# Five more norms take their rows by way of DRAM: memory, x, first feed-forward, between the blocks, second feed-forward

## The chip, the core and the metric

The kernel runs on one core of a Trainium2 chip. The metric is the device time of one execution in microseconds (us). The engines of the core are PE (TensorE, matrix products into PSUM), DVE (VectorE), ACT (ScalarE), POOL (GpSimd) and SP (SyncE, here a queue of weight loads). ACT and POOL issue DMAs too, each on its own queue. Every engine works through its instructions in a fixed order and waits on semaphores.

## The reference

Two transformer blocks over 512 rows of 1024 values in float32, one batch. The first block has a mixer (attention and a gated recurrence), cross attention to 256 memory rows and a feed-forward; the second has a gated convolution, a state-space branch and a gated feed-forward. Each part begins with an RMS norm, and this is the piece that matters here:

```python
def rmsnorm(x, g):
    xf = x.astype(jnp.float32)
    y = xf * lax.rsqrt(jnp.mean(xf * xf, axis=-1, keepdims=True) + EPS)
    return (y * g.astype(jnp.float32)).astype(x.dtype)
```

Five of these norms are touched: that of the memory, that of x at the start, the one ahead of the first feed-forward, the one between the blocks, and the one ahead of the second feed-forward.

## The kernel before

Activations lie transposed in SBUF: 128 of the 1024 columns on the partitions, the 512 rows along the free axis, eight tiles for one activation. A product in float32 is made of three matmuls in a reduced format, of the high and low parts of both sides: `mm3`, L150 to L152. A tile of a product, `gemm_tile`, is 8 column blocks x 3 = 24 matmuls of 128x512 into one PSUM slot of the pool `acc`, which has three slots. Weights come on SP's queue into `wr` (three buffers); ACT casts the high part `wh` (L138), DVE subtracts to get the low part `wl` (L139), and PE uses both. The cast of a later weight waits for PE to finish the tile that used the buffer.

A norm's factor is needed as a row: the scale of row r stands in column r of R, the same on all partitions, since DVE multiplies tiles of 128x512 by it. ACT squares the tiles and DVE adds them (`sqa`); PE sums over the partitions with one-column products (`col_sum`, L234), so that the sums of 512 rows stand as four columns of 128; DVE scales them (`rv`, L240) and POOL takes the power -1/2 (`rc`, L242). Then there are two ways from four columns to a row on all partitions:

- `row_bc` (L245 to L251): one 128x128 matmul per column against the identity (L249), then an ACT copy from PSUM to R.
- `row_far` (L253 on): one small transpose on PE (L256), an ACT copy to `rt` (L258), a DMA on ACT's queue to DRAM, `rd` (L260), and a DMA on POOL's queue that reads it back to all 128 partitions.

`row_far` is already used for the mixer's and the state-space branch's norms (their rows are Rh and Rg); the five norms of this case use `row_bc`.

In the products that follow a norm in the two feed-forwards the activations go in unnormed, since a row's factor can be applied to the product; so PE may start such tiles before R is there, and DVE multiplies the tile in PSUM by R when it reads it (L715, L1207, L1211). That read gives the PSUM slot back. For the x norm DVE multiplies h itself by R (L335), then ACT casts its high part xh and DVE makes its low part xl (L212, L213), and PE needs these.

The order of each engine is fixed at build by a scheduler: `tc.high_priority(-n)` lets instructions stand later in the order than their place in the code; `LATE`, `X2`, `X3` and the like are such numbers. `tc.issue_after(x)` holds an instruction behind another one.

In the second feed-forward the norm is made in two halves of 256 rows (`r3(cl, w)` over `parts`), each with its own column sums and row.

## Time and profile before

| | |
|---|---|
| time, median of 3 runs | 1896.86 us (1894.96 to 1898.19) |
| profiled execution, its own time | 1897.12 us |
| its span | 1895.3 us |
| around the span | 1.8 us |
| mean granted clock of PE, as a share of full speed | 0.998 |
| busy: PE, DVE, ACT, POOL | 1876.6, 1192.4, 843.7, 134.2 us |

The span reaches from the first instruction to the last of one profiled execution. Busy time is the sum of the instructions of an engine; a PE that is busy for nearly the whole span can only be made faster by taking work from it or by filling its gaps.

### The profile page before, as it was taken

Reading aid. Unit: us, or ns where it says so; the run is one execution under the profiler, and the core shown is the slowest. Engines: PE = TensorE matmul, PEld = TensorE weight load, DVE = VectorE, ACT = ScalarE, POOL = GpSimd, SP = SyncE. Lnnn points to the kernel's source line nnn. Section 1 sums busy time; section 2 is a strip of 40 time slices with the busy share of each in tenths; the row PEclk is TensorE's granted clock in tenths of the full one; section 3 lists DMA queues with packets and bytes.
Section 4 is the critical chain, followed back from the end, with each engine's and each line's share of the span. In section 5 each row is a group of like instructions: output and inputs, shape, how many; then the busy total and the mean of one; then the engine's idle time right before and its main releaser. Section 6 shows DMA issues by size and latency. Waiting matters only on the chain.

```text
span 1895.3 us, 24243 instructions
## 1 busy us (share of the span) xinstructions
PE 1876.6 (99%) x9313; PEld 1546.5 (82%) x9313; DVE 1192.4 (63%) x1837; ACT 843.7 (45%) x1364; POOL 134.2 (7%) x251
## 2 busy tenths in 40 slices
PE   9999999999999999999999999999999999999998
PEld 8787776878888888877888888888888998888887
DVE  6744756665442344467889889579998675423444
ACT  6524547444431243348545653445335553322231
POOL 1001110000000000011100110100000014000000
PEclk9999999999999999999999999999999999999999
DMA  7312222312233223334333433333345446223331
GB/s 259 137 56 101 67 79 73 106 56 89 89 100 98 93 99 111 108 92 132 126 109 123 124 128 100 115 102 123 105 139 188 153 133 177 93 97 100 97 103 67
DMA packets 65435, 210.65 MB, mean 111 GB/s; under 512 B 8884, under 2 KB 10720, under 8 KB 65320
## 3 DMA queue, kind: packets, MB, share of 16 engines
q1 hardware_dynamic: 52384, 177.27, 29.1%
q0 software_dynamic: 8672, 24.47, 4.6%
q10 hardware_dynamic: 4264, 7.37, 1.1%
q8 instruction: 73, 1.20, 0.3%
q14 instruction: 42, 0.34, 0.1%
HBM read 198.45 MB, written 10.66 MB: 110 GB/s over the span
## 4 chain that ended last, share of the span: by engine, by line
PE 93%; DVE 3%; DMA 1%; ACT 1%; issue 1%; POOL 0%; SPq 0%; DVEq 0%; POOLq 0%; ACTq 0%
PE acc L150 26%; PE acc L152 26%; PE acc L151 26%; PE pb L960 1%; PE pa L490 1%; PE pa L150 1%; PE pa L152 1%; PE pb L150 1%; PE pb L152 1%; PE pa L151 1%; PE pb L151 1%; PE pb L585 1%; PE pa L930 1%; DMA wr<-w_xk 1%; PE pb L557 1%
## 5 line engine op out<-in xcount | busy, mean ns | idle before, releaser
L138 ACT CAST wh<-wr 128x1024 fp32r<-128x1024 f32 x313 | 328.7, 1051 | 701.1 <-PE acc L151 512.7
L139 DVE TENSOR_TENSOR wl<-wr,wh 128x1024 fp32r<-128x1024 f32 x313 | 382.9, 1224 | 290.8 <-ACT wh L138 288.6
L150 PE MATMUL acc<-yh,wh 128*128 128x512 f32 (+1 forms) x1112 | 432.6, 389 | 0.4 <-DVE so L1008 0.3
L152 PE MATMUL acc<-yh,wl 128*128 128x512 f32 (+1 forms) x1112 | 431.5, 388 | 0.0
L151 PE MATMUL acc<-yl,wh 128*128 128x512 f32 (+1 forms) x1112 | 429.7, 386 | 0.0
L152 PE MATMUL acc<-xh,wl 128*128 128x512 f32 (+1 forms) x832 | 314.2, 378 | 0.3 <-DVE wl L139 0.3
L150 PE MATMUL acc<-xh,wh 128*128 128x512 f32 (+1 forms) x832 | 313.3, 378 | 0.3 <-DVE h L628 0.3
L151 PE MATMUL acc<-xl,wh 128*128 128x512 f32 (+1 forms) x832 | 313.4, 377 | 0.0
L150 PEld LDWEIGHTS acc<-yh,wh 128*128 128x128 f32 x1112 | 209.4, 188 | 42.4 <-issue 1.4
L152 PEld LDWEIGHTS acc<-yh,wl 128*128 128x128 f32 x1112 | 209.4, 188 | 42.1 <-issue 1.5
L151 PEld LDWEIGHTS acc<-yl,wh 128*128 128x128 f32 x1112 | 209.3, 188 | 41.4 <-issue 0.6
L851 DVE SCALAR_TENSOR_TENSOR cv<-gp,vec,cv 128x512 f32<-128x512 f32 x240 | 178.2, 750 | 5.9 <-ACT cv L849 3.0
L152 PEld LDWEIGHTS acc<-xh,wl 128*128 128x128 f32 x832 | 157.1, 189 | 28.8 <-issue 2.4
L150 PEld LDWEIGHTS acc<-xh,wh 128*128 128x128 f32 x832 | 156.8, 189 | 28.4 <-ACT xh L212 0.9
L151 PEld LDWEIGHTS acc<-xl,wh 128*128 128x128 f32 x832 | 156.9, 189 | 27.0 <-issue 1.3
L150 PE MATMUL acc<-uh,wh 128*128 128x512 f32 x256 | 99.6, 389 | 0.0
L151 PE MATMUL acc<-ul,wh 128*128 128x512 f32 x256 | 99.6, 389 | 0.0
L152 PE MATMUL acc<-uh,wl 128*128 128x512 f32 x256 | 99.6, 389 | 0.0
L715 DVE SCALAR_TENSOR_TENSOR t<-acc,R 128x512 f32<-128x512 f32 x32 | 22.0, 691 | 79.4 <-PE acc L152 78.5
L242 POOL TENSOR_TENSOR rc<-rv,mhalf 128x4 f32<-128x4 f32 (+2 forms) x19 | 23.5, 1235 | 606.2 <-DVE rv L240 521.0
L152 PEld LDWEIGHTS acc<-uh,wl 128*128 128x128 f32 x256 | 48.1, 188 | 10.0
L151 PEld LDWEIGHTS acc<-ul,wh 128*128 128x128 f32 x256 | 48.1, 188 | 9.9
(433 smaller groups left out, 2448.1 us busy)
## 6 DMA issues: line engine op xcount, KB each, us to landing
wr<-w SPq DMA_DIRECT2D x64, 512.0 KB, 3.7
wr<-w_gu SPq DMA_DIRECT2D x44, 512.0 KB, 3.4
wr<-w_out SPq DMA_DIRECT2D x24, 512.0 KB, 3.5
wr<-w_dn SPq DMA_DIRECT2D x22, 512.0 KB, 3.4
wr<-w_xs SPq DMA_DIRECT2D x16, 512.0 KB, 3.5
wr<-w_glu SPq DMA_DIRECT2D x16, 512.0 KB, 3.6
ab<-acsd POOLq DMA_DIRECT2D x32, 256.0 KB, 3.8
wr<-w_z SPq DMA_DIRECT2D x16, 512.0 KB, 4.1
```

What stands on the lines that cost most here:

```text
L138: A.copy(out=hi[:, :n], in_=raw[:, :n])
L139: V.tensor_tensor(out=lo[:, :n], in0=raw[:, :n], in1=hi[:, :n].bitcast(F32), op=ALU.subtract)
L150: T.matmul(out=ps, lhsT=lh, rhs=rh, start=start, stop=False)
L151: T.matmul(out=ps, lhsT=lh, rhs=rl, start=False, stop=False)
L152: return T.matmul(out=ps, lhsT=ll, rhs=rh, start=False, stop=stop)
L242: G.tensor_tensor(out=r[:, :nt], in0=v[:, :nt], in1=mhalf[:, :nt], op=ALU.pow)
L490: T.matmul(out=ps[:, j * 64:(j + 1) * 64], lhsT=k_[:, j * P:(j + 1) * P], rhs=qv[:, j, :, 1, :], start=True, stop=True)
L557: T.transpose(out=pt[:, i * P:(i + 1) * P], in_=Sx[:, i * P:(i + 1) * P], identity=ident)
L585: m = T.matmul(out=ps, lhsT=fq[p][es_, sl], rhs=fk[p][es_, 0:n], start=True, stop=True)
L715: V.scalar_tensor_tensor(out=t, in0=ps, scalar=0.0, in1=R, op0=ALU.max, op1=ALU.mult)
L851: yield V.scalar_tensor_tensor(out=o, in0=gp[:, t:t + S], scalar=cw(t), in1=o, op0=ALU.mult, op1=ALU.add)
L930: T.matmul(out=ps[:, 0:256], lhsT=Bt[:, c, :], rhs=xw[:, c].rearrange("p r d -> p (r d)"), start=True, stop=True)
```

## The change

Five places go from `row_bc` to `row_far` or to a way like it.

- Memory: `Rm` comes by `row_far` with two columns.
- x: `norm_fin` has an argument `far`, and is called with it here.
- First feed-forward: the column sums stand earlier in the order (`FARL` in place of `LATE`), and the transpose is held behind the fifth mark of the first tile (`first_tile`).
- Between the blocks: the transpose of `r1` and its DMA to DRAM (`rows1`) stand at the start of a much earlier part; where R1 is needed, a DMA on ACT's queue reads it back.
- Second feed-forward: the two halves become one norm over all four columns, by `row_far`.

The cross attention's norm is written anew with `norm_col`, and still uses `row_bc`.

```diff
--- before.py
+++ after.py
@@ -36,6 +36,7 @@
 LATE2 = 15
 LATE3 = 100
 X0 = 10
+FARL = 10
 RMARK = 3
 X1 = 0
 X2 = 30
@@ -258,26 +259,39 @@
         A.copy(out=t[0:nt], in_=ps[0:nt, 0:P])
         d = dram.tile([8, P], F32, tag="rd", name="rd", bufs=4)
         nc.scalar.dma_start(out=d[0:nt], in_=t[0:nt])
+        n = nt // len(dst)
         for i, x in enumerate(dst):
-            G.dma_start(out=x, in_=d[4 * i:4 * i + 4].rearrange("a b -> (a b)").unsqueeze(0).partition_broadcast(P))
+            G.dma_start(out=x, in_=d[n * i:n * i + n].rearrange("a b -> (a b)").unsqueeze(0).partition_broadcast(P))
         return dst
 
-    def norm(srcs, n, nt, gain=None, eps=EPS, pl=None, rtag="R", ms=mA, late=0):
-
-        ac = nrm.tile([P, S], F32, tag="sqa", name="sqa")
-        for k, s in enumerate(srcs):
-            sq_acc(ac[:, :nt * P], k, s, 1.0 if gain is None else gain(k))
-        return norm_fin(ac, n, nt, eps, pl, rtag, ms, late)
-
-    def norm_fin(ac, n, nt, eps=EPS, pl=None, rtag="R", ms=mA, late=0):
+    def norm_fin(ac, n, nt, eps=EPS, pl=None, rtag="R", ms=mA, late=0, far=False):
 
         pl = pl or nrm
         R = pl.tile([P, nt * P], F32, tag=rtag, name=rtag, bufs=1)
         with tc.high_priority(-late):
             r = rsqrt_col(col_sum(ac, nt, ms), nt, n, eps)
         with tc.high_priority(-2 * late):
-            A.copy(out=R, in_=row_bc(r, nt, ms))
+            if far:
+                row_far(r, nt, [R], ms)
+            else:
+                A.copy(out=R, in_=row_bc(r, nt, ms))
         return R, r
+
+    def norm_col(srcs, ms, late):
+
+        ac = nrm.tile([P, S], F32, tag="sqa", name="sqa")
+        for k, s in enumerate(srcs):
+            sq_acc(ac, k, s)
+        with tc.high_priority(-late):
+            return rsqrt_col(col_sum(ac, 4, ms), 4, D)
+
+    def first_tile(src, xs, r, R, ms):
+
+        marks = []
+        ps = gemm_tile(src, xs, marks=marks)
+        with tc.issue_after(marks[4].ins):
+            row_far(r, 4, [R], ms)
+        return ps
 
     emem = es_mem
 
@@ -323,13 +337,13 @@
         with tc.high_priority(400):
             rm = rsqrt_col(col_sum(ac, 2), 2, D)
         with tc.high_priority(-X3):
-            A.copy(out=Rm, in_=row_bc(rm, 2))
+            row_far(rm, 2, [Rm])
         ax = nrm.tile([P, S], F32, tag="sqa", name="sqa")
         for k in range(8):
             sq_acc(ax, k, h[k])
         for n in range(8):
             V.tensor_tensor(out=mk[n // 2][:, n % 2, :], in0=mk[n // 2][:, n % 2, :], in1=Rm, op=ALU.mult)
-        R, rc = norm_fin(ax, D, 4, pl=pmx, late=X3)
+        R, rc = norm_fin(ax, D, 4, pl=pmx, late=X3, far=True)
         xs = []
         for k in range(8):
             V.scalar_tensor_tensor(out=h[k], in0=h[k], scalar=vcol("norm_mix_g", k), in1=R, op0=ALU.mult, op1=ALU.mult)
@@ -642,7 +656,10 @@
         pc = ec.enter_context(pool("pc", 2, reuse_waits="tile"))
         pcy = ec.enter_context(pool("pcy", 8, reuse_waits="tile"))
         xs = [split_act(h[k], vcol("norm_x_g", k)) for k in range(8)]
-        R, _ = norm(h, D, 4, pl=pc, ms=mC, late=LATE)
+        R = pc.tile([P, S], F32, tag="R", name="R", bufs=1)
+        r = norm_col(h, mC, LATE)
+        with tc.high_priority(-2 * LATE):
+            A.copy(out=R, in_=row_bc(r, 4, mC))
         ys = []
 
         def split(t, lpool, ltag, lbufs, tag, bufs):
@@ -706,11 +723,13 @@
         pc = ec.enter_context(pool("pff", 2, reuse_waits="tile"))
         ph2 = ec.enter_context(pool("phid", 16, reuse_waits="tile"))
         xs = [split_act(h[k], vcol("norm_ff_g", k)) for k in range(8)]
-        R, _ = norm(h, D, 4, pl=pc, ms=mC, late=LATE)
+        R = pc.tile([P, S], F32, tag="R", name="R", bufs=1)
+        r = norm_col(h, mC, FARL)
         for grp in range(2):
             hid = []
             for n in range(16):
-                ps = gemm_tile([(a["w1"][grp * 16 + n], 8)], xs)
+                src = [(a["w1"][grp * 16 + n], 8)]
+                ps = gemm_tile(src, xs) if grp + n else first_tile(src, xs, r, R, mC)
                 t = pc.tile([P, S], F32, tag="t", name="t")
                 V.scalar_tensor_tensor(out=t, in0=ps, scalar=0.0, in1=R, op0=ALU.max, op1=ALU.mult)
                 t2 = pc.tile([P, S], F32, tag="t2", name="t2")
@@ -1008,6 +1027,14 @@
                 V.tensor_tensor(out=so[n], in0=so[n], in1=ps, op=ALU.add)
                 V.scalar_tensor_tensor(out=so[n], in0=t, scalar=1.0, in1=so[n], op0=ALU.add, op1=ALU.mult)
 
+
+    rows1 = dram.tile([4, P], F32, tag="rows1", name="rows1")
+    with tc.high_priority(-LATE3):
+        ps = mC()
+        T.transpose(out=ps[0:4, 0:P], in_=r1, identity=ident)
+        t = nrm.tile([8, P], F32, tag="sq", name="rt")
+        A.copy(out=t[0:4], in_=ps[0:4, 0:P])
+        nc.scalar.dma_start(out=rows1, in_=t[0:4])
     early = []
     for i, w in enumerate(ew):
         ps = gemm_tile([(w, 8)], xr) if i else eps_[0]
@@ -1080,7 +1107,7 @@
         nc.sync.dma_start(out=t, in_=hd_[k])
         h.append(t)
     R1 = pt_.tile([P, S], F32, tag="Rm", name="R1", bufs=1)
-    A.copy(out=R1, in_=row_bc(r1, 4))
+    nc.scalar.dma_start(out=R1, in_=rows1.rearrange("a b -> (a b)").unsqueeze(0).partition_broadcast(P))
     for n in range(8):
         ps = gemm_tile([(a["w_pw"][n], 8)], cs_)
         t = pt_.tile([P, S], F32, tag="pw", name="pw")
@@ -1116,14 +1143,15 @@
             V.scalar_tensor_tensor(out=xs[k][1][:, cl], in0=h[k][:, cl], scalar=g, in1=xs[k][0][:, cl].bitcast(F32),
                                    op0=ALU.mult, op1=ALU.subtract)
 
-    def r3(cl, w):
+    def r3():
         ac = nrm.tile([P, S], F32, tag="sqa", name="sqa")
-        for k in range(8):
-            sq_acc(ac[:, :w], k, h[k][:, cl])
+        for cl in parts:
+            for k in range(8):
+                sq_acc(ac[:, cl], k, h[k][:, cl])
         with tc.high_priority(-X2):
-            r = rsqrt_col(col_sum(ac[:, :w], w // P), w // P, D)
+            r = rsqrt_col(col_sum(ac, 4), 4, D)
         with tc.high_priority(-2 * X2):
-            A.copy(out=R3[:, cl], in_=row_bc(r, w // P))
+            row_far(r, 4, [R3])
 
     acs = out2(parts[0], HF)
     x3(parts[0], HF, acs, X0)
@@ -1157,8 +1185,7 @@
         for n, ps in zip(order, gu_tiles(order[:3]) + [gemm_tile([(a["w_gu"][n], 8)], xs) for n in order[3:NEARLY]]):
             early[n] = act.tile([P, S], F32, tag="xl", name="early")
             A.copy(out=early[n], in_=ps)
-        for cl in parts:
-            r3(cl, HF)
+        r3()
 
         def gu(n):
             return early[n] if n in early else gemm_tile([(a["w_gu"][n], 8)], xs)
```

How the instructions stand, at three places. First DVE at the x norm. Before (h0 to h2 are tiles of x, R is the x norm's row, `vec` the gains, Rm the memory's row, mk the memory's keys):

```order
L331 TENSOR_TENSOR mk_136<-mk_136,Rm_482 128x256 x2
L240 TENSOR_SCALAR rv_531<-pa_526 128x4 [waits PE_49]
L139 TENSOR_TENSOR wl_664<-wr_661,wh_663 128x1024 [waits DMAHW3_49,Activation_49]
L139 TENSOR_TENSOR wl_682<-wr_679,wh_681 128x1024 [waits DMAHW4_49,Activation_49]
L139 TENSOR_TENSOR wl_700<-wr_697,wh_699 128x1024 [waits DMAHW5_49,Activation_49]
L335 SCALAR_TENSOR_TENSOR h0_141<-h0_141,vec_90,R_525 128x512 [waits Activation_49]
L335 SCALAR_TENSOR_TENSOR h1_142<-h1_142,vec_90,R_525 128x512 [waits DMAHW6_49]
L335 SCALAR_TENSOR_TENSOR h2_143<-h2_143,vec_90,R_525 128x512 [waits DMAHW0_49]
L139 TENSOR_TENSOR wl_718<-wr_715,wh_717 128x1024 [waits DMAHW6_49,Activation_49]
L213 TENSOR_TENSOR xl_543<-h0_141,xh_542 128x512 [waits Activation_49]
```

There the first multiply by R follows on three weights' `wl`. The same place of DVE after the change:

```order
L345 TENSOR_TENSOR mk_135<-mk_135,Rm_482 128x256 x2
L345 TENSOR_TENSOR mk_136<-mk_136,Rm_482 128x256 x2
L241 TENSOR_SCALAR rv_534<-pa_529 128x4 [waits PE_49]
L140 TENSOR_TENSOR wl_722<-wr_719,wh_721 128x1024 [waits DMAHW7_49,Activation_49]
L185 TENSOR_TENSOR wn_751<-wr_749,wn_751 128x8x32 [waits DMAHW0_49,Activation_49]
L140 TENSOR_TENSOR wl_821<-wr_818,wh_820 128x1024 [waits DMAHW1_49,Activation_49]
L349 SCALAR_TENSOR_TENSOR h0_141<-h0_141,vec_90,R_528 128x512 [waits DMASW5_49]
L349 SCALAR_TENSOR_TENSOR h1_142<-h1_142,vec_90,R_528 128x512
L349 SCALAR_TENSOR_TENSOR h2_143<-h2_143,vec_90,R_528 128x512
L140 TENSOR_TENSOR wl_856<-wr_853,wh_855 128x1024 [waits DMAHW3_49,Activation_49]
L214 TENSOR_TENSOR xl_547<-h0_141,xh_546 128x512 [waits Activation_49]
```

The first multiply by R waited for ACT's copy and now waits for a DMA of POOL's queue (DMASW5); the column factor `rv` stands behind the multiplies by Rm as before, and a weight's `wl` stands between the multiplies and the first `xl`.

Second, PE at the x norm's row. Before (acc tiles are the memory's values, `rc` the four columns):

```order
L150 MATMUL acc_659<-wh_663,mh_159 128x512
L249 MATMUL pa_535<-ident_129,rc_533 128x128 [waits PE_49,Pool_49]
L151 MATMUL acc_659<-wl_664,mh_159 128x512
L249 MATMUL pa_535<-ident_129,rc_533 128x128
L152 MATMUL acc_659<-wh_663,ml_160 128x512
L150 MATMUL acc_660<-wh_663,mh_155 128x512 [waits PE_49,Activation_49]
L249 MATMUL pa_535<-ident_129,rc_533 128x128
L151 MATMUL acc_660<-wl_664,mh_155 128x512
L249 MATMUL pa_535<-ident_129,rc_533 128x128
L152 MATMUL acc_660<-wh_663,ml_156 128x512
```

After, on PE where the transpose stands:

```order
L152 MATMUL acc_663<-wl_686,mh_169 128x512
L153 MATMUL acc_663<-wh_685,ml_170 128x512
L257 MATMUL pa_538<-ident_129,rc_536 4x128 [waits Pool_49]
L151 MATMUL acc_664<-wh_685,mh_165 128x512
L152 MATMUL acc_664<-wl_686,mh_165 128x512
L153 MATMUL acc_664<-wh_685,ml_166 128x512
```

One transpose stands between two products of the memory's values where four matmuls stood among them. After, on PE again, the end of the memory's values and the first products of x:

```order
L151 MATMUL acc_664<-wh_721,mh_189 128x512
L152 MATMUL acc_664<-wl_722,mh_189 128x512
L153 MATMUL acc_664<-wh_721,ml_190 128x512
L189 MATMUL acc_754<-xh_546,wn_751 64x512 [waits Activation_49]
L151 MATMUL acc_817<-xh_546,wh_820 128x512 [waits PE_49]
L189 MATMUL acc_754<-xl_547,wn_751 64x512 [waits DVE_49]
L189 MATMUL acc_754<-xh_551,wn_751 64x512 [waits Activation_49]
```

From the transpose to the first product of `xh` there are 30 matmuls, and the third product of x is the first that reads `xl`.

Third, DVE at the second feed-forward. Before (`early` are three finished tiles of the product, copied to SBUF, the acc tiles three further ones that are still in PSUM, called A, B and C in order; tile D takes the slot of A):

```order
L139 TENSOR_TENSOR wl_13211<-wr_13208,wh_13210 128x1024 [waits DMAHW4_49,PE_49,Activation_49]
L240 TENSOR_SCALAR rv_13059<-pa_13056 128x2 [waits PE_49,Pool_49]
L139 TENSOR_TENSOR wl_13245<-wr_13242,wh_13244 128x1024 [waits DMAHW5_49,PE_49,Activation_49]
L1207 TENSOR_TENSOR t_13078<-early_12993,R3_12171 128x512 [waits Activation_49]
L1211 TENSOR_TENSOR t2_13081<-early_12995,R3_12171 128x512
L1207 TENSOR_TENSOR t_13088<-early_12997,R3_12171 128x512
L1212 TENSOR_TENSOR t2_13081<-t2_13081,t_13078 128x512 [waits DVE_49,Activation_49]
L1211 TENSOR_TENSOR t2_13122<-acc_13091,R3_12171 128x512
L1207 TENSOR_TENSOR t_13160<-acc_13129,R3_12171 128x512 [waits DVE_49]
```

There the multiplies by R3 wait for ACT, whose copy makes it. The same place of DVE after the change:

```order
L241 TENSOR_SCALAR rv_13055<-pa_13050 128x4 [waits PE_49,Pool_49]
L140 TENSOR_TENSOR wl_13210<-wr_13207,wh_13209 128x1024 [waits DMAHW1_49,Activation_49]
L1201 STREAM_TRANSPOSE ht_13200<-x2_0_11815 128x512 [waits DVE_49]
L140 TENSOR_TENSOR wl_13244<-wr_13241,wh_13243 128x1024 [waits DMAHW2_49,PE_49,Activation_49]
L1201 STREAM_TRANSPOSE ht_13278<-x2_1_11817 128x512 [waits DMAHW5_49,Activation_49]
L140 TENSOR_TENSOR wl_13288<-wr_13285,wh_13287 128x1024 [waits DMAHW3_49,PE_49,Activation_49]
L1234 TENSOR_TENSOR t_13077<-early_12999,R3_12177 128x512 [waits DMASW5_49]
L1238 TENSOR_TENSOR t2_13080<-early_13001,R3_12177 128x512
L1234 TENSOR_TENSOR t_13087<-early_13003,R3_12177 128x512
L1239 TENSOR_TENSOR t2_13080<-t2_13080,t_13077 128x512 [waits DVE_49,Activation_49]
L1238 TENSOR_TENSOR t2_13121<-acc_13090,R3_12177 128x512
L1234 TENSOR_TENSOR t_13159<-acc_13128,R3_12177 128x512 [waits DVE_49]
```

The two `rv` of the halves became one; the multiplies by R3 now wait for a DMA of POOL's queue, and stand in the same order among themselves, with the read of A (acc_13090) fifth. A further weight's `wl` and two transposes of x2 stand ahead of them.

## Rows read from the trace of the kernel before

**Rows 1.** The page: busy time of the engines, and the chain that ended last.

```profile
PE 1876.6 (99%) x9313; PEld 1546.5 (82%) x9313; DVE 1192.4 (63%) x1837; ACT 843.7 (45%) x1364; POOL 134.2 (7%) x251
...
PE 93%; DVE 3%; DMA 1%; ACT 1%; issue 1%; POOL 0%; SPq 0%; DVEq 0%; POOLq 0%; ACTq 0%
```

**Rows 2.** What PE waits for, longest first: us in total, times, longest.

```profile
PE pa L922 <- ACT Ct L829: 3.2, 1, 3.2
PE pc L803 <- ACT dtc L804: 1.5, 1, 1.5
```

**Rows 3.** Timeline of PE, 57.5 to 59: start us, us, engine, line, instruction.

```profile
57.14 0.39 PE L150 MATMUL acc<-wh,mh 128*128 128x512 f32 x1
...
58.28 0.39 PE L152 MATMUL acc<-wh,ml 128*128 128x512 f32 x1
58.50 0.40 PE L188 MATMUL acc<-xh,wn 128*64 128x512 f32 x1
```

**Rows 4.** Busy time in two stretches; the number before the last two is PE's granted clock.

```profile
852.00:856.00 4.00, 4.00 (x12) 3.14 (x11) 3.32 (x5) 1.79 (x3) 2.83 (x7) 0.57 0.49 152
872.00:876.00 4.00, 3.73 (x13) 2.90 (x14) 1.82 (x4) 3.13 (x7) 0.54 (x1) 0.57 0.40 144
```

**Rows 5.** Timeline of PE, 36 to 66: the x norm's row.

```profile
47.35 0.39 PE L150 MATMUL acc<-wh,mh 128*128 128x512 f32 x1
47.58 0.38 PE L249 MATMUL pa<-ident,rc 128*128 128x128 f32 x2
...
49.63 0.39 PE L150 MATMUL acc<-wh,mh 128*128 128x512 f32 x1
```

**Rows 6.** Timeline of PE, 164 to 166.5: a transpose of another norm.

```profile
164.50 0.39 PE L152 MATMUL acc<-wh,xl 128*128 128x512 f32 x1
164.72 0.27 PE L256 MATMUL pc<-ident,rc 128*8 128x128 f32 x1
...
165.06 0.40 PE L151 MATMUL acc<-wl,xh 128*128 128x512 f32 x1
```

**Rows 7.** Timeline of ACT: the start of rt in two norms.

```profile
165.03 0.26 ACT L258 COPY rt<-pc 8x128 f32<-8x128 f32 x1 [6.81 <-PE pc L256]
...
1119.15 0.26 ACT L258 COPY rt<-pc 4x128 f32<-4x128 f32 x1 [1.43 <-PE pc L256]
```

**Rows 8.** Timeline of DVE: the first use of the same two rows.

```profile
170.99 1.44 DVE L533 SCALAR_TENSOR_TENSOR mix<-mix,vec,Rh 128x512 f32<-128x512 f32 x2 [0.29 <-DMA Rh<-rd]
...
1126.90 0.75 DVE L990 SCALAR_TENSOR_TENSOR zs<-zs,vec,Rg 128x512 f32<-128x512 f32 x1 [0.31 <-DMA Rg<-rd]
```

**Rows 9.** Timeline of DVE, 36 to 76: the first use of the x norm's R.

```profile
50.22 2.08 DVE L335 SCALAR_TENSOR_TENSOR h<-h,vec,R 128x512 f32<-128x512 f32 x3 [1.04 <-ACT R L279]
52.22 1.22 DVE L139 TENSOR_TENSOR wl<-wr,wh 128x1024 fp32r<-128x1024 f32 x1
53.35 0.68 DVE L213 TENSOR_TENSOR xl<-h,xh 128x512 fp32r<-128x512 f32 x1
```

**Rows 10.** Timeline of ACT, 478 to 486: first feed-forward.

```profile
482.07 0.59 ACT L279 COPY R<-pc 128x512 f32<-128x512 f32 x1 [1.62 <-PE pc L249]
...
485.80 1.05 ACT L138 CAST wh<-wr 128x1024 fp32r<-128x1024 f32 x1
```

**Rows 11.** Timeline of ACT, 1549 to 1570: a weight's cast, second feed-forward.

```profile
1555.89 1.05 ACT L138 CAST wh<-wr 128x1024 fp32r<-128x1024 f32 x1 [2.61 <-PE acc L151]
```

**Rows 12.** Timeline of PE, 1430 to 1434: behind the row of r1.

```profile
1431.93 0.47 PE L150 MATMUL acc<-yh,wh 128*128 128x512 f32 x1 [0.33 <-DVE so L1008]
```

**Rows 13.** Timeline of DVE, 1424 to 1437: the addition that PE waits for.

```profile
1431.10 0.68 DVE L1008 TENSOR_TENSOR so<-so,acc 128x512 f32<-128x512 f32 x1
```

**Rows 14.** Timeline of DVE, 1549 to 1570: first uses of R3.

```profile
1558.12 0.68 DVE L1207 TENSOR_TENSOR t<-early,R 128x512 f32<-128x512 f32 x1
...
1560.52 0.68 DVE L1211 TENSOR_TENSOR t<-acc,R 128x512 f32<-128x512 f32 x1
```

**Rows 15.** Timeline of PE, 1549 to 1566: the start of tile D.

```profile
1561.84 0.39 PE L150 MATMUL acc<-yh,wh 128*128 128x512 f32 x1
```

## Prediction

> **What bounds it now.** I read the page first: PE is busy for 99% of the span and 93% of the chain that ended last is PE's own work [rows 1]. So whatever PE no longer does is gained, and whatever PE stands still for is lost; nothing else counts. Next the list of what PE waits for: the two longest waits of the whole run are 3.2 and 1.5 us [rows 2], so a new wait of a few microseconds would stand out. Then the timeline of PE: five starts lie 1.14 us apart, so a 128x512 matmul starts every 0.227 us [rows 3], a tile of 24 takes 5.45, and the products of the first norm's x (L188) begin at 58.50. Last the granted clock. It stands at its upper level, 2.4 GHz, nearly everywhere, but in the 4 us from 852 it is 0.57 and in the 4 us from 872 also 0.57 [rows 4]: mostly the lower level, 1.2 GHz. These stretches come right behind the two longest waits. So a wait of 1.5 us or more has cost here a further 4 x (1 - 0.57) = 1.7 us.
>
> The profiled execution took 1897.12 us, 0.26 above the median of the three runs; the sums below start from it. Within 0.2% (3.8 us) two kernels can't be told apart.
>
> **What PE saves.** Four matmuls that spread a norm's row lie between the product starts at 47.35 and 49.63, six starts apart: 2.28 - 6 x 0.227 = 0.92 us [rows 5]. The transpose that takes their place exists already elsewhere: from 164.50 to 165.06 it adds 0.56 - 2 x 0.227 = 0.11 us [rows 6]. So a norm of four columns gives PE 0.8 us, the memory's two columns about 0.3. Five norms give 0.3 + 4 x 0.8 = 3.5 us, if all else stays hidden.
>
> **What the row costs in time.** Before, R was there one ACT copy after the matmuls. In the way by DRAM, ACT copies the transposed row (rt), sends it to DRAM, and POOL's queue brings it back to all partitions. From the start of rt to the first DVE instruction that reads the row: 165.03 to 170.99, 6.0 us, and 1119.15 to 1126.90, 7.75 us [rows 7, 8]. These are my two bounds for R; in the first DVE stood idle for it, so it is an arrival, and I take the middle, 6.9. (The Trainium skill, "DMA: Bandwidth & Descriptors", section "Anatomy of one DMA — SWDGE (gpsimd) path", gives a transfer a fixed cost of about 2.0 us, mostly the receipt of the write. Two in a row, with the copy, make an estimate of 4.5 us; the trace shows more. By that figure both stalls below were about 2.4 us shorter, and the time would be about 1901.) The question at each place is then what PE still has to do in those 7 us.
>
> **Memory and x norms.** In the new order PE has 30 matmuls between the x norm's transpose and the first product that needs it: 30 x 0.227 = 6.8 us. rt starts 0.3 behind the transpose (164.72 and 165.03 [rows 6, 7]), so R comes 6.3 to 8.05 us behind it. But R is not yet what PE reads. DVE first multiplies three tiles of h by R, 0.69 each, then splits a weight, 1.22, then makes xl, 0.68: 3.97 us [rows 9]. PE therefore reads xl 10.3 to 12.0 us behind the transpose and has been out of work for 3.4 to 5.2, middle 4.35. Two products that read only xh fall into this gap (0.45). The memory's row and the x row together save 0.3 + 0.8 = 1.1. Net: 4.35 - 0.45 - 1.1 = +2.8 us, bounds +1.9 and +3.65. A second way to lose here: the x norm's rv stands on DVE behind eight multiplies by Rm, which now wait for DRAM too. I price this at nothing, since PE works on the memory's values meanwhile, with up to 1 us more as the bound. The cover before was these values: R was ready while 30-odd of their products were left.
>
> **First feed-forward.** The third tile after the first needs the PSUM slot that the first gives back after DVE has multiplied it by R. Before it began at the cast at 485.80 [rows 10], now 0.8 earlier, 485.0. The first tile ends two tiles and a transpose earlier, 474.0; the cast of 1.05 [rows 11] and rt follow, R is there at 481.1 to 482.8, the slot is free 0.69 later. 1.5 us are to spare at worst: no stall, -0.75 us.
>
> **Between the blocks.** The block of four matmuls goes, but right behind it PE waited 0.33 us for DVE, until 1431.93 [rows 12]: the slot that it needs is freed by an addition that DVE reaches at 1431.10 [rows 13], in an unbroken row of work that began with another norm's row. Without the block PE comes 0.9 earlier and waits that much longer. I take 0; the other bound is -0.8. The transposed row is fetched long before use, and loading R1 on ACT's queue delays only the residual, which PE does not need for two tiles.
>
> **Second feed-forward, now in one piece.** This is the largest term. PE meets the transpose at the end of tile B and has one tile, C, left (5.45 us and 0.11); tile D needs the slot of tile A. On ACT, rt stands behind a cast of 1.05 that begins when B ends [rows 11]. So R3 is there 1.05 + 6.0 to 7.75 = 7.05 to 8.8 us behind B's end. DVE then does three multiplies of early tiles, a product and the multiply that reads A: 0.6 apart (four from 1558.12 to 1560.52 [rows 14]), the last 0.68, 3.1 us. A's slot is free 10.15 to 11.9 us behind B's end; PE stands still for 4.6 to 6.3, middle 5.5. Before, that multiply was at 1560.52, done at 1561.20, and tile D began at 1561.84 without a wait [rows 15]: 0.64 us to spare. Against it stand 0.9 us of saved matmuls. Net 5.5 - 0.9 = +4.6 us, bounds +3.7 and +5.4.
>
> **The clock.** Both gaps are over 1.5 us. For the second I take the full 1.7 us of [rows 4]. In the first, PE is led by DVE for 7 us more (some twelve instructions of 0.6 to 0.7), and at the lower clock it loses little that it would not wait for: 0.5. Bounds: nothing for either, and 1.7 for each.
>
> **Sum.** +2.8 - 0.75 + 0 + 4.6 + 1.7 + 0.5 = +8.85 us. 1897.12 + 8.85 = 1905.97, and 0.26 less to the median: 1905.7 us, slower by 0.47%. All the low ends together: 1.9 - 0.8 - 0.8 + 3.7 = +4.0, 1900.9; all the high ones, with the extra 1 us: 3.65 + 1 - 0.75 + 0 + 5.4 + 3.4 = +12.7, 1909.6.
>
> **Rivals.**
> 1. *Everything is hidden: faster.* Then only the saved matmuls count, -3.5 and 0.8 of it lost between the blocks: 1894.2 (1893.4 with it). It decides at the latency of the row. At the x norm R would have to come within 6.8 - 3.97 = 2.9 us of the transpose; at the second feed-forward within 5.56 - 3.1 = 2.5 us of B's end, of which the cast takes 1.05. No row of this trace came back in under 6.0. For it speaks only that I read the order of five engines by hand and could have a slot wrong. 0.07.
> 2. *Only the second feed-forward stalls.* If PE finds enough at the x norm, this place gives -1.1 instead of +2.8: -1.1 - 0.75 + 4.6 + 1.7 = +4.45, 1901.3. Against it: the products that need x stand in a fixed order with nothing behind them that could go ahead. 0.1.
> 3. *Only the x norm stalls.* If A's slot is freed by something earlier, the second feed-forward gives -0.9: 2.8 - 0.75 - 0.9 + 0.5 = +1.65, 1898.5, no difference to be told. Three tiles share the slots, so I hold it unlikely. 0.1.
> 4. *More waits than I see.* The first feed-forward's 1.5 us to spare vanish if the row takes 10 us there, or the longer wait between the blocks lowers the clock too (1.7): 1907 to 1910. 0.08.
> 5. My forecast, both stalls, 1901 to 1909: 0.65.
>
> The likeliest gives the time. Leaving out the first and third rival and the upper end of the fourth, the range is 1899.5 to 1909.5. Faster has rival 1, 0.07; the same has rival 3 and the low edge of 2, 0.11; slower the rest, 0.82.
>
> **What will show it.** In the list of PE's waits two new entries must stand above all that is there now, but for the 3.2 us: a product of the second feed-forward that waits some 5.5 us for DVE's multiply by R3 near 1565, and L188-type products near 60 that wait about 4 us in two or three pieces for xh and xl. The granted clock must be near 0.5 for a few microseconds after the first of them. PE's matmul count must fall by 13. From 75 to 470 every instruction should stand 2 to 3.5 us later than before, from 490 to 1540 about 1.5 to 2.5, and at the end 8 to 9. I am wrong if the row comes back in 3 us, if PE finds the slot of tile A free, or if DVE's multiply of early tiles does not wait for R3.

## The result

The changed kernel takes 1907.28 us (median of 4 runs, 1906.86 to 1908.53), the kernel before 1897.09 (4 runs): a ratio of 1.0053, 95% interval 1.004 to 1.0065. It is 10.2 us slower; the forecast was 8.85 us, 1905.7 us with a range of 1899.5 to 1909.5.

### The profile after

The page of the changed kernel: PE is as busy as before [rows 1], and the span is 10.0 us longer. The matmul count falls by 31, from 9313 to 9282: 18 products that spread a row went and 5 transposes came, 13 instructions fewer, but the profile counts each of the 18 twice (x2 in [rows 5]).

```profile
span 1905.3 us, 24190 instructions
...
PE 1877.3 (99%) x9282; PEld 1545.0 (81%) x9282; DVE 1192.8 (63%) x1836; ACT 841.4 (44%) x1363; POOL 137.2 (7%) x254
```

What PE waits for in the changed kernel, longest first (us in total, times, longest), against [rows 2]:

```profile
PE acc L151 <- ACT uh L213: 5.3, 1, 5.3
PE pa L941 <- ACT Ct L848: 2.4, 1, 2.4
PE acc L189 <- ACT xh L213: 2.1, 1, 2.1
PE acc L189 <- DVE xl L214: 1.7, 1, 1.7
PE pc L822 <- ACT dtc L823: 1.5, 1, 1.5
...
PE acc L151 <- DVE so L1027: 1.2, 1, 1.2
```

Three entries are new: 5.3 us ahead of a product of the second feed-forward, and 2.1 and 1.7 at the x norm's products (L189 is L188 of before). Their sum is 9.1 us. The wait for Ct is 2.4 us where it was 3.2, and the wait for DVE's addition `so` 1.2 where it was 0.3.

Where the 10 us arise is seen by laying the two timelines side by side. Every weight's low part is made by one DVE subtraction (L139, after L140), 313 of them in the same sequence; the start of the k-th in one trace less its start in the other is the delay at that point:

| start of such a subtraction before, us | what lies between it and the one above | later in the changed kernel, us | change, us |
|---|---|---|---|
| 52.2 | the memory's norm, x's first products | -1.55 | |
| 432.6 | x norm's row, mixer, cross attention | +5.67 | +7.2 |
| 497.7 | first feed-forward's row | +4.90 | -0.8 |
| 829.7 | first feed-forward | +4.90 | 0 |
| 994.7 | start of the state-space part | +3.69 | -1.2 |
| 1540.8 | the rest of it, row between the blocks, projections | +3.74 | 0 |
| 1601.0 | second feed-forward's row | +9.88 | +6.1 |

A place named below by a time, such as "the delay at 126", is a start in the kernel before. The delay is level over hundreds of microseconds and jumps at five places. The -1.55 at 52.2 and part of the jump behind it belong together: work that stood 1.55 us earlier reached the same wait sooner. So the memory and x norms together give +5.7.

Timeline of PE at the x norm in the changed kernel (against [rows 3]):

```profile
50.75 0.27 PE L257 MATMUL pa<-ident,rc 128*4 128x128 f32 x1
...
57.48 0.39 PE L153 MATMUL acc<-wh,ml 128*128 128x512 f32 x1
59.95 0.45 PE L189 MATMUL acc<-xh,wn 128*64 128x512 f32 x1 [2.08 <-ACT xh L213]
62.36 0.69 PE L189 MATMUL acc<-xl,wn 128*64 128x512 f32 x1 [1.73 <-DVE xl L214]
...
65.41 0.63 PE L151 MATMUL acc<-xh,wh 128*128 128x512 f32 x1
65.83 0.63 PE L152 MATMUL acc<-xl,wh 128*128 128x512 f32 x1
```

The transpose stands at 50.75 and PE has run out of the memory's values at 57.7; after 2.08 and 1.73 us of standing still it reads xl at 62.36. From there the products start 0.43 us apart (65.41 and 65.83) and not 0.227. The windows of the changed kernel show why (the number before the last two is the granted clock; then the busy share of the DMA engines, and GB/s):

```profile
56.00:60.00 4.00, 1.92 (x10) 1.26 (x8) 2.73 (x4) 2.80 (x6) 0.00 (x0) 1.00 1.01 326
60.00:64.00 4.00, 2.27 (x6) 1.27 (x7) 4.00 (x6) 1.92 (x4) 0.00 (x0) 0.63 0.39 130
64.00:68.00 4.00, 4.00 (x11) 2.86 (x10) 4.00 (x8) 1.85 (x3) 0.00 (x0) 0.51 0.10 38
...
1568.00:1572.00 4.00, 1.77 (x4) 1.50 (x5) 4.00 (x8) 2.27 (x5) 0.53 (x1) 0.72 0.50 167
```

At both new gaps the granted clock falls to its lower level, as it does at the two waits of [rows 4], and products run at that level behind the gap. Timeline of PE at the second feed-forward, the last product of tile C and the first one of tile D, against [rows 15]:

```profile
1564.57 0.39 PE L153 MATMUL acc<-yh,wl 128*128 128x512 f32 x1
1570.23 0.77 PE L151 MATMUL acc<-yh,wh 128*128 128x512 f32 x1 [5.27 <-ACT uh L213]
```

The same place on ACT, against [rows 11]: the cast that begins when tile B ends, and rt behind it.

```profile
1559.18 1.05 ACT L139 CAST wh<-wr 128x1024 fp32r<-128x1024 f32 x1 [5.11 <-PE acc L152]
1560.13 0.25 ACT L259 COPY rt<-pa 4x128 f32<-4x128 f32 x1
```

And on DVE, against [rows 14]: the last weight's low part ahead of the multiplies, the first multiply by R3, and the multiply that reads tile A.

```profile
1565.85 1.22 DVE L140 TENSOR_TENSOR wl<-wr,wh 128x1024 fp32r<-128x1024 f32 x1 [3.45 <-ACT wh L139]
1566.99 0.68 DVE L1234 TENSOR_TENSOR t<-early,R 128x512 f32<-128x512 f32 x1
...
1569.39 0.69 DVE L1238 TENSOR_TENSOR t<-acc,R 128x512 f32<-128x512 f32 x1
```

Tile A is read until 1570.08 and D begins at 1570.23: the wait is for A's slot. The list of waits puts it down to ACT's `uh`, which ended at 1570.13; but D does not read uh, and run 4 below gives D another slot and the wait is gone.

From the start of rt to the first multiply are 6.86 us, but the multiply did not wait for the row: it stands right behind the weight's low part, which DVE worked at from 1565.85. The row had landed by then, about 4.0 us behind its issue at 1562.17. From the view of tile R, 1555 to 1572:

```profile
L264 POOL DMA_DIRECT2D R<-rd x1: 578/578/578, 1562.2 to 1562.2; - x1
DMA to landing us min/median/max: 4.0/4.0/4.0
```

So the row itself took 6.0 us from the start of rt, and the weight's low part, whose cast on ACT began only near the end of tile C (1564.77), set the last 0.9 us of the wait. It does so wherever this order stands: in the eight profiles that have it (the changed kernel, runs 2, 4, 5, 7 and 9 to 11) the first multiply comes 6.86 or 6.87 us behind rt, though the row landed 5.6 to 6.2 us behind it.

### The profile page after: what moved, and what is told of

Its sections match the earlier page's. It is cut to its first block, busy times and chain, and to the rows that moved or that the text cites. A ratio compares the mean times of both kernels' runs of the same rounds, so it can differ in the third digit from the quotient of the medians.

```text
span 1905.3 us, 24190 instructions
## 1 busy us (share of the span) xinstructions
PE 1877.3 (99%) x9282; PEld 1545.0 (81%) x9282; DVE 1192.8 (63%) x1836; ACT 841.4 (44%) x1363; POOL 137.2 (7%) x254
## 4 chain that ended last, share of the span: by engine, by line
PE 93%; DVE 3%; ACT 1%; issue 1%; DMA 1%; POOL 0%; SPq 0%; DVEq 0%; POOLq 0%; ACTq 0%
PE acc L151 26%; PE acc L153 26%; PE acc L152 26%; PE pb L979 1%; PE pa L504 1%; PE pa L151 1%; PE pa L153 1%; PE pb L151 1%; PE pa L152 1%; PE pb L153 1%; PE pb L152 1%; PE pa L949 1%; PE pb L599 1%; PE pc L235 1%; PE pb L571 1%
## 5 line engine op out<-in xcount | busy, mean ns | idle before, releaser
L139 ACT CAST wh<-wr 128x1024 fp32r<-128x1024 f32 x313 | 328.2, 1050 | 715.9 <-PE acc L152 530.0
L140 DVE TENSOR_TENSOR wl<-wr,wh 128x1024 fp32r<-128x1024 f32 x313 | 382.6, 1224 | 295.1 <-ACT wh L139 292.1
```

Source lines behind the costliest of these rows:

```text
L139: A.copy(out=hi[:, :n], in_=raw[:, :n])
L140: V.tensor_tensor(out=lo[:, :n], in0=raw[:, :n], in1=hi[:, :n].bitcast(F32), op=ALU.subtract)
```

## The experiments

All of them are kernels made from the changed one or from the one before; differences are given to the kernel before as it ran on the same chip, with the 95% interval of the ratio turned into microseconds.

**1. The second feed-forward's row back.** `r3` as before: two halves, `row_bc`.

```diff
-        r3()
+        for cl in parts:
+            r3(cl, HF)
```

> The changed kernel with the second feed-forward's norm back in two halves and on row_bc. If the loss there belongs to this place alone (a wait of 5.3 us for a PSUM slot, and a lower clock behind it, 6.15 us by the offsets of the weights' steps between the two traces), the time falls by 6.1 us to about 1901.1 and PE's longest wait is the 2.4 us of the state-space part. Rival: the late row only makes visible what the earlier late rows had shifted (DVE and POOL work bunched up); then part of it stays and the time falls by less than 4 us.

1901.23 us, +4.5 to the kernel before (2.5 to 6.1). PE does not wait for `uh`; the delay at the place goes from +3.94 to +3.95. The place costs 10.2 - 4.5 = 5.7 us by the times and 6.1 by the trace, and no part of it stays.

**2. The memory's and the x norm's rows back.**

```diff
-            row_far(rm, 2, [Rm])
+            A.copy(out=Rm, in_=row_bc(rm, 2))
...
-        R, rc = norm_fin(ax, D, 4, pl=pmx, late=X3, far=True)
+        R, rc = norm_fin(ax, D, 4, pl=pmx, late=X3)
```

> The changed kernel with the memory's and the x norm's rows back on row_bc. By the offsets of the weights' steps these two places lose 5.7 us, 4.65 in a gap of PE, 2.6 in the lower clock behind it, less some savings: about 1901.6. PE has no wait near 60 and the clock stays at its upper level there. Rival: part of the loss near 60 is the later x work in itself (DVE is the pace), and returns only in part: above 1903.

1902.62 us, +5.9 (3.4 to 7.8). No wait near 60. The two rows cost 10.2 - 5.9 = 4.3 us by the times; the difference of the runs 1 and 3 gives 4.8. The time lies between what was expected and its rival. The trace sides with the first: the delay is -0.8 at 52.2 and -0.7 at 126, so nothing of the 5.7 stays. This execution lost time elsewhere: the lower clock lasted about twice as long as in the changed kernel at two later waits (the last section), and the second feed-forward's place cost 7.2 and not 6.1.

**3. Both back.** The edits of 1 and 2 together.

> The changed kernel with both of these back, so that only the first feed-forward and the row between the blocks go by DRAM. By the offsets: first feed-forward -0.8, state-space part -1.2, between the blocks 0: 1895.0, 2 us below the kernel before (0.1%). Rival: the -1.2 in the state-space part comes from the delay of all earlier work (weights that lie ready longer), not from the moved row; then 1896.2.

1896.46 us, -0.3 (-2.8 to +0.6). The effects of the two places add up (4.3 + 5.7 = 10.0 of 10.2). The 2 us of gain that were expected lie within the interval and are not shown by the time. In its trace the run began late, 3.55 us behind at 52.2: PE waited 2.1 us near 19 for the sum of the memory's squares, which stood on ACT behind the cast of a weight that landed late, and the clock fell there. From 52.2 on the delays fall by 0.8 at the first feed-forward and by 2.6 in the state-space part.

**4. Another slot for tile D.**

```diff
-    def gemm_tile(src_blocks, xs, n=S, marks=None):
+    def gemm_tile(src_blocks, xs, n=S, marks=None, ps=None):
...
-        ps = acc.tile([P, S], F32, tag="acc", name="acc")
+        ps = ps or acc.tile([P, S], F32, tag="acc", name="acc")
...
-            return early[n] if n in early else gemm_tile([(a["w_gu"][n], 8)], xs)
+            return early[n] if n in early else gemm_tile([(a["w_gu"][n], 8)], xs, ps=mB() if n in (3, 25) else None)
```

> The changed kernel with tiles D and E of the second feed-forward in two PSUM buffers of another pool (pb), which is idle there, in place of two of acc's three slots; the row still comes by DRAM. If the wait is for the slot, PE does not wait there and the clock does not fall: -5.3 -1.0 to -1.7 us, so 1900.0 to 1901.0, and the place gains about 0.9 against the kernel before. Rival: PE waits for the row in another way (the weight's low part behind the multiplies on DVE, or the next slots): then a gap of 2 us or more stays, above 1903.

1900.57 us, +3.8 (2.3 to 5.7). Timeline of PE, the start of tile D in the other pool:

```profile
1564.31 0.39 PE L151 MATMUL pb<-yh,wh 128*128 128x512 f32 x1
```

D begins without a wait while the row is still under way (in this run it landed near 1565.6); the delay at the place goes from +3.25 to +2.47. So the place gains 0.8 us when PE has a slot, where it lost 6.1: the row's way itself costs nothing there. The slot is what PE waited for.

**5. Products that nobody reads, in both gaps.** Shown for the second feed-forward; at the x norm 30 products of 128x256 likewise behind the memory's values.

```diff
+        def fill(after, cnt, l, r):
+            ps = mB()
+            with tc.issue_after(after[-1].ins):
+                for i in range(cnt):
+                    T.matmul(out=ps, lhsT=l, rhs=r, start=True, stop=True)
...
+            if n == 3:
+                fill(lastC, 20, xs[7][0][:, 0:P], xs[7][0])
```

> The changed kernel with products that nobody reads in PE's two gaps: 30 of 128x256 (3.6 us) behind the memory's values and 20 of 128x512 (4.5 us) ahead of tile D. They make nothing earlier: xl and the slot come when they came. If the clock falls because PE stands still, it stays at its upper level at both places and what it cost comes back: 2.6 us near 65 and 1.3 us near 1572, so 1907.3 - 3.9 = 1903.4. Rival: the clock falls there for another reason (the load of DVE and ACT, the DMAs), or DVE is the pace near 65 in any case: then the time stays within 1.5 us of 1907.3, and at the lower clock the useless products make it longer.

1906.13 us, +8.1 (5.5 to 10.2), 2.0 less than the changed kernel by the differences; 3.9 were expected. Timeline of PE at both gaps:

```profile
56.83 3.75 PE L361 MATMUL pb<-mh 128*128 128x256 f32 x30
...
62.51 0.45 PE L189 MATMUL acc<-xl,wn 128*64 128x512 f32 x1 [1.69 <-DVE xl L215]
62.79 0.40 PE L189 MATMUL acc<-xh,wn 128*64 128x512 f32 x1
63.11 0.45 PE L189 MATMUL acc<-xl,wn 128*64 128x512 f32 x1
...
1563.47 4.69 PE L1201 MATMUL pb<-yh 128*128 128x512 f32 x20
1568.91 0.47 PE L151 MATMUL acc<-yh,wh 128*128 128x512 f32 x1 [0.75 <-ACT uh L214]
```

And the granted clock there:

```profile
60.00:64.00 4.00, 2.31 (x12) 1.08 (x12) 4.00 (x7) 2.02 (x5) 0.00 (x0) 1.00 0.29 96
64.00:68.00 4.00, 4.00 (x18) 2.73 (x17) 4.00 (x7) 1.86 (x3) 0.00 (x0) 1.00 0.12 47
...
1568.00:1572.00 4.00, 3.25 (x15) 2.56 (x15) 4.00 (x8) 2.07 (x4) 0.00 (x0) 1.00 0.27 106
```

The clock stays at its upper level at both places, so it is PE's standing still that lowered it in the changed kernel. At the second feed-forward the place now costs 7.20 - 2.41 = 4.8 us in place of 6.1: the clock was worth the 1.3 expected. At the x norm it was worth less than the 2.6: with the clock up, PE waits for xl again and again (62.51 to 63.11: pairs of starts 0.60 apart, where two products take 0.45). How much less is not sharp. Counted from 52.2 the place costs 6.45 in place of 7.29, 0.8 less, and the times leave 2.0 - 1.3 = 0.7. But in this run the row came 8.45 us behind rt and not 7.43, so that PE read xl at 62.51, hardly later than the 62.36 of the changed kernel, from an earlier start. In the changed kernel and the runs 1, 4 and 8 PE read xl at 62.36 to 62.91, and the delay at 126 was 5.5 to 6.0; here it is 4.0. By that 1.4 to 2.0 of the 2.6 came back. What is left is DVE's pace.

**6. Only the row between the blocks by DRAM,** on the kernel before.

```diff
+    rows1 = dram.tile([4, P], F32, tag="rows1", name="rows1")
...
-    A.copy(out=R1, in_=row_bc(r1, 4))
+    nc.scalar.dma_start(out=R1, in_=rows1.rearrange("a b -> (a b)").unsqueeze(0).partition_broadcast(P))
```

> The kernel before with only the row between the blocks sent by DRAM. If the moved ACT work in the state-space part brings the 1.2 us that the two traces show there, the wait of PE for Ct is 2.4 us in place of 3.2 and the time is 1.2 us less, 1895.6; where R1 is used nothing is gained, PE waits 1.2 us there for DVE's addition in place of 0.3. Rival, that of the prediction: no effect in the state-space part, 1896.8.

1896.67 us, -1.3 (-3.2 to 0.0). What PE waits for there:

```profile
PE pa L922 <- ACT Ct L829: 2.4, 1, 2.4
...
PE acc L150 <- DVE so L1008: 1.2, 1, 1.2
```

The wait for Ct is 2.4 us in place of 3.2 without any other edit, and the delay goes from +0.84 to -0.51 over that part; where R1 is used the whole saving is lost to the wait for `so`, 1.2 us. The time alone does not tell it from nothing: the interval reaches to 0.

**7. The rows by DRAM where PE has work meanwhile.** The edits of 2 and 4 together.

> The changed kernel with the memory's and the x norm's rows on row_bc and tiles D and E in the idle pool: the rows by DRAM stay at the first feed-forward, between the blocks and at the second feed-forward, where PE has work meanwhile. If the effects of the places add up: 1902.6 of the run with the x norm back, less the 6.7 us that the other slot brought: 1895.9, 0.9 us below the kernel before. Rival: the places don't add up and it is above 1897.

1894.51 us, -3.5 (-4.7 to -1.3): a little faster than the kernel before, by 0.2%; 0.9 us below it were expected. (Run again as number 11 below.)

**8. The second feed-forward's transpose earlier.**

```diff
-        with tc.high_priority(-2 * X2):
+        with tc.high_priority(-42):
             row_far(r, 4, [R3])
```

> The changed kernel with the second feed-forward's transpose 17 products earlier in PE's order, as soon as the power is there, and so ahead of the weight's cast on ACT. If the row's way is what PE waits for, the gap ahead of tile D shrinks from 5.3 us by about as much as rt starts earlier (3.6 us, some of it a wait of PE for the power), to 1 to 2 us, and the clock stays up: 1902.5 to 1903.5. Rival: something later than the row (the weight's low part that stood ahead of the multiplies on DVE, the way back on POOL's queue behind the transposes of x2) sets the end: the gap stays above 4 us and the time within 1.5 us of 1907.3.

1902.26 us, +4.3 (3.0 to 6.5). Timeline of PE, the transpose and the first product of D:

```profile
1556.27 0.27 PE L257 MATMUL pa<-ident,rc 128*4 128x128 f32 x1 [1.00 <-POOL rc L243]
...
1566.39 0.47 PE L151 MATMUL acc<-yh,wh 128*128 128x512 f32 x1 [0.28 <-ACT uh L213]
```

The same kernel's DVE, the first multiply by R3:

```profile
1563.14 0.69 DVE L1234 TENSOR_TENSOR t<-early,R 128x512 f32<-128x512 f32 x1 [0.35 <-DMA R<-rd]
```

rt starts 3.55 us earlier, at 1556.58; PE waits 1.00 for the power and 0.28 ahead of D, in place of 5.27. The place costs 4.66 - 3.75 = 0.9 us in place of 6.1. The first multiply still comes 6.56 us behind rt: here DVE does wait for the row. But the new order also puts the weight's low part that stood ahead of the multiplies behind them (it starts at 1567.35), so this run does not tell the row from that step. By the landing of the row in the changed kernel, 0.9 us ahead of the first multiply, an estimate is that the row alone would have made PE wait 4.4 of the 5.27 us; a run with only the low part moved was not made.

**9. The memory's row alone by DRAM,** on the version of number 7.

> The version with x back and another slot, with the memory's row alone sent by DRAM again. If the memory's row is harmless by itself, it saves PE 0.3 us and the x norm's matmuls, a little later in the order, still come long before x is needed: 1894.2, no gap near 60. Rival: the memory's row is what hurts, since rv of the x norm stands on DVE behind the multiplies by Rm: then PE waits near 50 or 60 and the time is above 1896.

1894.19 us, -3.4 (-4.6 to -1.1), beside 1894.12 of number 11 on the same chip. No gap near 60: by itself it does no harm, and saves nothing that can be measured.

**10. The x norm's row alone by DRAM,** on the version of number 7.

> The version with x back and another slot, with the x norm's row alone sent by DRAM again, the memory's by matmuls. Here 44 products stand between the transpose and the first product of xh, not 30, since rv no longer waits behind Rm. If the gap is the row's way less PE's work meanwhile, it shrinks by 14 x 0.227 = 3.2 us, from 4.65 to about 1.5 us, too short to lower the clock by much, and the place costs 1 to 2.5 us instead of some 5: 1895.5 to 1897. Rival: the x norm's way costs the same wherever the transpose stands, since DVE makes xh and xl one by one behind it: 1899 or more.

1895.39 us, -2.2 (-4.0 to -0.6), 1.3 above number 11. Timeline of PE:

```profile
47.26 0.27 PE L257 MATMUL pa<-ident,rc 128*4 128x128 f32 x1
...
58.17 0.45 PE L189 MATMUL acc<-xl,wn 128*64 128x512 f32 x1 [0.39 <-DVE xl L214]
...
59.91 0.45 PE L189 MATMUL acc<-xl,wn 128*64 128x512 f32 x1 [1.05 <-DVE xl L214]
```

The transpose stands 3.5 us earlier than in the changed kernel, and PE stands still for 0.39 and 1.05 at the products of x, in place of 2.08 and 1.73. Why it can stand earlier shows on DVE, at the x norm's scale factors: first the changed kernel, then this run.

```profile
49.35 0.16 DVE L241 TENSOR_SCALAR rv<-pa 128x4 f32<-128x4 f32 x1
```

```profile
41.67 0.15 DVE L241 TENSOR_SCALAR rv<-pa 128x4 f32<-128x4 f32 x1
```

With the memory's row by DRAM the adds of x's squares and the multiplies by Rm come later on DVE, and rv with them (51.12 in run 9). So most of the loss at the x norm needs both rows. The x norm's row alone still costs something: 1.3 us by the medians, 2.4 in the two profiled executions (a delay of +2.45 at 126, +0.09 in number 11). The expectation had the clock hardly fall; it fell here too:

```profile
60.00:64.00 4.00, 4.00 (x11) 2.75 (x12) 4.00 (x6) 2.22 (x5) 0.00 (x0) 0.62 0.57 174
```

In this run the power was ready at 42.92 and the transpose stood 4.3 us behind it; no run put it there, so whether the x norm's row can be hidden wholly stays open.

**11. Number 7 once more,** on the chip of 9 and 10.

> The version with x back and another slot once more, on the chip of the two others: 3.5 us below the kernel before, as measured (by 0.7 to 4.7). Rival: that was the chip or the executions, and it is less than 1.5 us.

1894.12 us, -3.5 (-4.7 to -1.3): the gain of number 7 again. In its trace the delays fall by 0.75 at the first feed-forward, 1.4 in the state-space part and 0.8 at the second feed-forward, 2.9 together.

## Why the prediction was right

The direction, the two stalls and their mechanism were as forecast; the size was 1.4 us short. That it was so little is partly luck: by the trace the memory and x norms cost 2.4 us more than the sum has, and the state-space part gave back 1.2 us that the sum does not have. For that reason the delays that the prediction named missed along the way: +5.7 and not 2 to 3.5 from 126 to 432, +4.9 and then +3.7 and not 1.5 to 2.5 up to 1540, +9.9 and not 8 to 9 at the end.

- **Memory and x norms**, +2.8 and 0.5 for the clock, 3.3 forecast: 5.7 by the trace, 4.3 to 4.8 by the times (runs 1 to 3). The gap itself was right: xl was read 4.65 us behind the end of the memory's values (4.35 forecast), with R 7.4 us behind rt. Mis-sized was what lies around it. The end of the memory's values moved by 0.8 and not 1.1. So PE's third product of x stands 3.4 us later than before (62.36 against 58.97), where the sum has 2.8. Behind that another 2.3 us were lost, where the sum has 0.5 for the clock: thirteen products stood 0.43 apart at the lower clock, worth 0.7 to 2.0 us (run 5), and the rest is DVE's pace, which the sum named and took as free. (The 3.97 us of DVE's work add up durations; by the starts of [rows 9] they are 3.8.)
- The step "30 products between transpose and x" was right as an order and blind as a cause. "A second way to lose here" was priced at nothing, since PE had work meanwhile. It is what made them 30: without the memory's row by DRAM there are 44, and the place costs 1.3 us by the times, 2.4 by the trace (run 10).
- **First feed-forward**, -0.75: -0.8 by the trace, no wait.
- **Between the blocks**, 0: at the place itself 0, by the mechanism named (1.2 us of waiting for `so` in place of 0.3). But the early transpose changed ACT's order in the state-space part, which the sum did not price: -1.2 by the trace, and -1.2 to -1.4 in runs 1, 4, 5, 6, 8, 10 and 11; -2.6 and -2.8 in runs 3 and 7, where the clock stayed up as well (below). Runs 2 and 9 have it too, -1.2 up to 870, but lost 1.8 and 1.7 again by 960: there the lower clock lasted longer (below). On ACT in the kernel before, from a table load to Ct:

```profile
866.06 1.28 ACT L950 ACT_TABLE_LOAD   x1
...
867.89 0.97 ACT L949 ACTIVATE ab<-ab,acc__6632 128x128 f32<-128x128 f32 x3
868.77 0.56 ACT L822 COPY xp<-acc 128x512 f32<-128x512 f32 x1
...
871.59 0.63 ACT L829 ACTIVATE Ct<-Ct 128x512 f32<-128x512 f32 x1
```

The same stretch of the changed kernel, 4.9 us later at this point:

```profile
870.32 1.28 ACT L969 ACT_TABLE_LOAD   x1
...
872.15 0.46 ACT L925 COPY Btok<-pa 128x384 f32<-128x384 f32 x1
...
874.04 1.28 ACT L848 ACT_TABLE_LOAD   x1
875.33 0.63 ACT L848 ACTIVATE Ct<-Ct 128x512 f32<-128x512 f32 x1
```

The copy `xp` no longer stands ahead of Ct, nor do two of the three `ab` steps at 867.89, and Btok's copy now follows the first table load instead of preceding it: Ct comes at 875.33, 1.2 us sooner than 871.59 + 4.9.
- **Second feed-forward**, +4.6 and 1.7: 6.1 by the trace, 5.7 to 6.2 by the times. The gap was 5.27 (5.5 forecast), the clock 1.3. That the gap fits is in part luck. The prediction would have been wrong, it said, if DVE's multiply of early tiles did not wait for R3, and it did not: the row was there 6.0 us behind the start of rt, the low end of the forecast, and the weight's low part, which the sum leaves out, filled the time to 6.86, close to the middle of 6.9. Without it the wait would have been 4.4, by the same estimate as at run 8.
- The rival "everything is hidden" failed at the point named: the rows that DVE waited for in the changed kernel came 5.92 (first feed-forward) to 7.43 us (x norm) behind the start of rt. Of the rival "more waits than I see" nothing came: PE has no wait at the first feed-forward, and behind the 1.2 us between the blocks the clock stayed at its upper level. The rival that the second feed-forward finds a slot came true when one was given to it (run 4).

## What to carry to other kernels

A broadcast by way of DRAM takes work off PE, 0.8 us a norm here, and puts a latency in its place, 5.8 to 8.6 us from the start of rt to DVE's first use of the row at the places of this change. Count the products that PE still has between the transpose and the first one that needs the row, and the free PSUM slots, which ran out first at the second feed-forward. Where there were not enough of either, it cost 4 to 6 us. At the second feed-forward two more slots took all of it back, and the transpose 17 products earlier all but 0.9 us. Look too at what the build's order puts ahead of the first use of the row: there a weight's low part, not the row, came last. Two latencies in a row (the memory's row ahead of the x norm's) cost more than the two alone (4.3 to 4.8 us, against nothing and 1.3 by the times), since the second one's start is moved past the work that would have hidden it.

## What the runs showed of the hardware that was not expected

The same wait of 1.5 us near 850 (dtc, the same in all 13 profiles) was followed by the lower clock in eleven of them and not in two, the runs 3 and 7. Windows of run 7, against [rows 4]:

```profile
850.00:854.00 4.00, 4.00 (x21) 2.88 (x20) 3.19 (x6) 2.39 (x6) 2.36 (x5) 1.00 0.52 121
854.00:858.00 4.00, 4.00 (x20) 3.28 (x19) 3.68 (x6) 3.23 (x6) 0.58 (x4) 1.00 1.01 273
```

Behind the wait of 2.4 us for Ct the lower clock lasted about twice as long in the runs 2 and 9 as in the others. Windows of run 2; in the kernel before the second one has 1.00:

```profile
872.00:876.00 4.00, 4.00 (x22) 2.71 (x24) 2.29 (x5) 2.86 (x7) 0.54 (x1) 0.50 0.20 66
876.00:880.00 4.00, 4.00 (x22) 2.77 (x20) 2.76 (x5) 3.47 (x8) 1.07 (x2) 0.76 0.21 66
```

So what a wait costs behind it is not fixed: at dtc some 1.4 us or nothing from one execution to the next, at Ct 1.7 to 1.8 us more or not. It fits with this that a kernel's own times spread: 26 runs of the kernel before lay between 1895.27 us, with a mean granted clock of 0.999, and 1900.20 us, with 0.995. They have no trace, so that is not shown.

In run 5 the granted clock stayed at its upper level through a wait of 1.69 us (ahead of 62.51), behind 30 products that nobody reads; in run 10, without such products, it fell behind waits of 0.39 and 1.05 us.

In four runs the x norm's row came later than the upper bound of 7.75 us that the prediction took for a row. In the runs 1, 4, 5 and 8 DVE first used it at 58.6 to 59.0, 8.0 to 8.6 us behind rt, though rt started 0.4 to 0.9 us earlier than in the changed kernel (58.49, 7.43 us). What holds it there is not shown; the DMA engines were busy throughout the window from 56 to 60 in the changed kernel (a share of 1.01).
